# A transformer kernel: the last mixer in reusable 8 KB buffers, operands at a fixed distance in SBUF, and the scatter moved within the expert

## The chip, the cores and the metric

One core of a Trainium2 chip runs the kernel. The metric is the device time in microseconds, taken as the median of three runs. Each run is one launch that goes from inputs in HBM to the output in HBM.

## The reference

256 tokens of width 1024 go through two blocks, all in float32. The first block has two layers; each is a SwiGLU FFN (hidden width 2816), a mixer and a second FFN. The second block has a third mixer and a mixture of 32 experts.

```python
for i in range(2):
    x = x + 0.5 * swiglu(rmsnorm(x), ffn1[i])
    x = x + (gla_mixer if i == 0 else sb_mixer)(rmsnorm(x))
    x = x + 0.5 * swiglu(rmsnorm(x), ffn2[i])
h = rmsnorm(x)                       # second block
proj = rms_norm(h) @ w_in            # conv input, two gates, q, k, v
h = h + concat([short_conv(...), diff_attention(...)]) @ w_out
hn = rms_norm(h)
# each token: the best of 4 groups, the best 2 of its 8 experts
for e in range(32):
    y += (silu(hn @ gate[e]) * (hn @ up[e]) * comb[:, e]) @ down[e]
return h + y
```

Every weight is used once, so 393 MB have to come from HBM: 180 tiles of 1 MB for the dense part (four FFNs, three mixers) and 192 tiles, six for each expert (four of gate and up, two of down).

## The kernel before

**The dense part.** Everything lies transposed, channels on the 128 partitions and 256 tokens along them. Each float32 operand is cut into a high and a low float32r part, and `mm3` makes a product of three matmuls: high weights with the high and the low part of the tokens, low weights with the high part. The tokens are `hhi` and `hlo`. A weight tile is loaded into `raw`, ScalarE copies the high part to `whi`, VectorE the rest to `wlo`; each of the three names has a ring of four buffers of 128 x 2048. The class `Feed` goes through a list of all tiles (`weight_plan`) in the order of use. `gu` matmuls take `hhi`, `hlo`; down takes `ahi`, `alo` (the activated gate times up) and accumulates in `acc`; projections of the mixers are `pj`; `pv` are the value projections, in which the tokens are the weights and the weight tile is streamed. The output projections `acco` take `ohi`, `olo` in the first two mixers and `mhi`, `mlo` in the third.

**Where the operands lie.** Tiles get their place in SBUF one after the other in the order in which the code makes them, and a pool starts behind the pools that are open. In the built program `whi` and `wlo` lie at multiples of 512 bytes. Every operand of a product is a slice at a multiple of 512 bytes in its tile, so the distance from weights to moving operand, modulo 512, is the same for all products of one pair of tiles:

| moving operand | where | distance modulo 512 |
|---|---|---|
| `hhi`, `hlo` | all `gu` and `pj` | 480 |
| `ahi`, `alo` | down of FFNs 1 to 3 | 192 |
| `ahi`, `alo` | down of FFN 4 (the pool `late` is open) | 64 |
| `ohi`, `olo` | output projection of the first mixer | 384 |
| `ohi`, `olo` | output projection of the second mixer | 192 |
| `mhi`, `mlo` | output projection of the third mixer | 64 |
| the weight tile, with `hhi` as weights | `pv` | 32 |

**The expert part.** An expert's tile isn't split: it goes as it is into any free buffer of 8 KB a partition, and the matmuls are float32. `Feed.load` issues the loads, all on SP's queue and in the list's order; each waits on the queue until its buffer is free. After the last dense tile, the buffers come one after the other: the four of `raw` as the last dense tiles are split, `whi` and `wlo` as the last output projection leaves them (`feed.done`), four `wx` of a pool that opens when the third mixer's pool is closed, and `h32` and `xT` when the router has read them. From then on each expert tile that has been used hands its buffer back:

```python
w = feed.take(("gx", "w_exp", e, j))
...
feed.add([w])
```

The third mixer `mix2` has the tensors `q2`, `k2`, `sq2`, `vt2`, `yT`, `oT`, `mhi`, `mlo`, four `p`, `u` and small ones in its own pool. In the expert loop `gate_up(e)` makes the gate and up products of the tokens gathered for expert e (`gx`, from `xg`), `act(s)` transposes and activates, `down(e, a)` gives `yy`, and `scatter(e - 1, ...)` adds the expert before to the accumulators with eight matmuls, after `gate_up(e)` is complete. The order on each engine is the order of the code (`manual_schedule`).

Of the kernel before, what the change touches and what calls it, by code (L numbers as in the profile page):

```python
# [14 lines left out]
OP = mybir.AluOpType  # L15
# [10 lines left out]
NE = 32  # L26
SL = 32
# [164 lines left out]
class Feed:  # L192
# [5 lines left out]
    def __init__(self, nc, pool, wts, plan):  # L198
        self.nc, self.pool, self.wts, self.plan = nc, pool, wts, plan
        self.M = sum(k[0] not in ("gx", "dx") for k in plan)  # L200
        self.raw, self.cut, self.free = {}, {}, []
        self.nl = self.ns = self.at = 0

    def part(self, name, dtype):

        return self.pool.tile([P, TW], dtype, name=name, tag=name, bufs=self.RING)
# [84 lines left out]
def body(ctx, tc, xin, small, cst, masks, groups, wts, out):  # L291
# [12 lines left out]
    ct = base.tile([P, cwid], F32, name="ct")  # L304
    g0 = base.tile([P, ND], F32, name="g0")
    feed = Feed(nc, base, wts, plan)
    nc.sync.dma_start(out=g0, in_=small[:, 0:ND])
# [15 lines left out]
    ones = base.tile([P, 2], F32, name="ones")  # L323
# [3 lines left out]

    hhi = base.tile([P, ND, T], F32R, name="hhi")
    hlo = base.tile([P, ND, T], F32R, name="hlo")
    ssq = base.tile([P, 2, 512], F32, name="ssq")  # L330
    rt = base.tile([P, 2], F32, name="rt")
    rb = base.tile([P, T], F32, name="rb")
# [278 lines left out]
    def gla(gnext):  # L611
        with tc.tile_pool(name="gla", bufs=1) as pool, tc.tile_pool(name="glaa", bufs=1, space=PS) as pacc:
# [332 lines left out]
    def mix2(gnext):  # L945
        with tc.tile_pool(name="mix", bufs=1) as pool:
            half2["pool"] = plate
            H4 = (P, 4, T)
            qk = [pool.tile(H4, F32, name=n) for n in ("q2", "k2")]
            sq = pool.tile(H4, F32, name="sq2")  # L950
            vt = pool.tile([P, 2, 512], F32, name="vt2")
            yT = pool.tile(H4, F32, name="yT")
            oT = pool.tile(H4, F32, name="oT")
            mhi = pool.tile([P, ND, T], F32R, name="mhi")
            mlo = pool.tile([P, ND, T], F32R, name="mlo")
            cb = pool.tile([P, 2, P], BF16, name="cb2")
            rb1, rbb = ssq[:, 1, :T], ssq[:, 1, T:]
            sel = pool.tile([2 * ND, ND * P], F32, name="sel")
            nc.sync.dma_start(out=sel, in_=groups)
            nlam = pool.tile([P, 4], F32, name="nlam")  # L960
            gq = pool.tile([P, 2], F32, name="gq")
            rt1 = pool.tile([P, 2], F32, name="rt1")
            nc.gpsimd.tensor_copy(cb[:, 0, :], ident)
            nc.gpsimd.tensor_copy(cb[:, 1, :], C("negc"))
            rb2 = rb[:, None, :].to_broadcast([P, 2, T])
            half = C("half")
            g1 = S("final_norm")

            def pair(b):
                return b.rearrange("p (s t) -> p s t", s=2)  # L970

            def stats2():
                ms = bank("ms")
                for k, src in ((0, ssq[:, 0, :]), (1, ssq2)):
                    for tb in range(2):
                        for h in range(2):
                            o = h * T + tb * P
                            mm(ms[:, 2 * k + tb:2 * k + tb + 1], lhsT=src[:, o:o + P], rhs=one, start=(h == 0), stop=(h == 1))

                v = pool.tile([P, 4], F32, name="v4")  # L980
                nc.vector.tensor_scalar(v[:, 0:2], ms[:, 0:2], 1.0 / D, EPS, op0=OP.mult, op1=OP.add)
# [694 lines left out]
```

## Time and profile before

| | before |
|---|---|
| median of three runs | 1607.97 us (1607.24 to 1608.25) |
| the profiled execution, its own time | 1605.98 us |
| its span, first to last instruction | 1603.8 us |
| TensorE busy | 1448.3 us, 90% |
| VectorE busy | 782.6 us, 49% |
| ScalarE busy | 570.1 us, 36% |
| DMA | 395.60 MB, 247 GB/s over the span |
| mean granted TensorE clock | 0.953 |

Busy is the time in which an engine runs at least one instruction. Matmuls overlap one another, so a matmul's duration (some 280 ns) is longer than the time from one start to the next; a busy share near 1 means that TensorE always has work, not that it works as fast as it can. The span is 2.2 us shorter than the execution's own time.

### The profile page before, as it was taken

Reading aid. Unit: us, or ns where it says so; the run is one execution under the profiler, and the core shown is the slowest. Engines: PE = TensorE matmul, PEld = TensorE weight load, DVE = VectorE, ACT = ScalarE, POOL = GpSimd, SP = SyncE. Lnnn points to the kernel's source line nnn. Section 1 sums busy time; section 2 is a strip of 40 time slices with the busy share of each in tenths; the row PEclk is TensorE's granted clock in tenths of the full one; section 3 lists DMA queues with packets and bytes.
Section 4 is the critical chain, followed back from the end, with each engine's and each line's share of the span. In section 5 each row is a group of like instructions: output and inputs, shape, how many; then the busy total and the mean of one; then the engine's idle time right before and its main releaser. Section 6 shows DMA issues by size and latency. Waiting matters only on the chain.

```text
span 1603.8 us, 31147 instructions
## 1 busy us (share of the span) xinstructions
PE 1448.3 (90%) x13785; PEld 1271.2 (79%) x13785; DVE 782.6 (49%) x1163; ACT 570.1 (36%) x708; POOL 52.8 (3%) x53
## 2 busy tenths in 40 slices
PE   8999999999999999999999999999996676676665
PEld 8999999999999999999999999998752332242322
DVE  6765677766566656563466556877310110110001
ACT  5444455454444544455554444544210000000000
POOL 0000013100000000000010000100000000000000
PEclk9999999999999999999999999999898888878888
DMA  7645544245544555543345555424999999999996
GB/s 288 240 183 187 188 158 159 98 179 198 200 174 154 225 190 189 184 171 120 132 141 210 202 178 185 157 89 150 421 423 424 424 424 424 423 424 423 424 424 283
DMA packets 56475, 395.60 MB, mean 247 GB/s; under 512 B 6401, under 2 KB 6657, under 8 KB 8977
## 3 DMA queue, kind: packets, MB, share of 16 engines
q1 hardware_dynamic: 56336, 393.57, 63.3%
q8 instruction: 110, 1.80, 0.4%
q14 instruction: 29, 0.23, 0.0%
HBM read 392.50 MB, written 1.05 MB: 245 GB/s over the span
## 4 chain that ended last, share of the span: by engine, by line
PE 66%; DMA 26%; DVE 4%; ACT 3%; issue 1%; SPq 0%; ACTq 0%
DMA wlo<-wts 12%; PE gu L442 10%; PE gu L440 10%; PE gu L441 10%; DMA raw<-wts 9%; PE acc L440 5%; PE acc L441 5%; PE acc L442 5%; DMA wx<-wts 4%; PE pj L440 3%; PE pj L441 3%; PE pj L442 3%; DMA xT<-wts 1%; DVE wlo L252 1%; PE gx L1473 1%; ACT whi L249 1%
## 5 line engine op out<-in xcount | busy, mean ns | idle before, releaser
L252 DVE TENSOR_TENSOR wlo<-raw,whi 128x2048 fp32r<-128x2048 f32 (+1 forms) x186 | 413.3, 2232 | 205.4 <-ACT whi L249 205.4
L440 PE MATMUL gu<-hhi,whi 128*128 128x256 f32 x1408 | 397.4, 282 | 6.9 <-ACT whi L249 6.9
L442 PE MATMUL gu<-hhi,wlo 128*128 128x256 f32 x1408 | 397.1, 282 | 1.5 <-DVE wlo L252 1.5
L441 PE MATMUL gu<-hlo,whi 128*128 128x256 f32 x1408 | 396.6, 282 | 0.0
L249 ACT ACTIVATE whi<-raw 128x2048 fp32r<-128x2048 f32 (+1 forms) x186 | 342.5, 1855 | 51.0 <-issue 40.9
L440 PEld LDWEIGHTS gu<-hhi,whi 128*128 128x128 f32 x1408 | 266.3, 189 | 6.9 <-ACT whi L249 6.9
L442 PEld LDWEIGHTS gu<-hhi,wlo 128*128 128x128 f32 x1408 | 266.3, 189 | 2.5 <-DVE wlo L252 2.5
L441 PEld LDWEIGHTS gu<-hlo,whi 128*128 128x128 f32 x1408 | 266.4, 189 | 0.0
L440 PE MATMUL acc<-ahi,whi 128*128 128x256 f32 x704 | 195.7, 278 | 0.0
L441 PE MATMUL acc<-alo,whi 128*128 128x256 f32 x704 | 195.4, 278 | 0.0
L442 PE MATMUL acc<-ahi,wlo 128*128 128x256 f32 x704 | 195.2, 277 | 0.0
L1510 DVE TENSOR_SCALAR pt<-ptb,ct 128x256 f32<-128x256 f32 x32 | 15.5, 484 | 306.4 <-PE ptb L1508 306.4
L1477 ACT ACTIVATE gs<-gx 128x256 f32<-128x256 f32 x32 | 12.3, 384 | 366.7 <-PE gx L1473 366.7
L480 ACT ACTIVATE sg<-gp 128x256 f32<-128x256 f32 x88 | 36.8, 418 | 294.4 <-DVE gp L479 289.8
L442 PEld LDWEIGHTS acc<-ahi,wlo 128*128 128x128 f32 x704 | 132.5, 188 | 0.0
L440 PEld LDWEIGHTS acc<-ahi,whi 128*128 128x128 f32 x704 | 132.4, 188 | 0.0
L441 PEld LDWEIGHTS acc<-alo,whi 128*128 128x128 f32 x704 | 132.1, 188 | 0.0
L440 PE MATMUL pj<-hhi,whi 128*128 128x256 f32 x416 | 120.2, 289 | 0.0
L441 PE MATMUL pj<-hlo,whi 128*128 128x256 f32 x416 | 118.5, 285 | 0.6 <-DVE hlo L391 0.6
L442 PE MATMUL pj<-hhi,wlo 128*128 128x256 f32 x416 | 118.1, 284 | 0.0
L1473 PE MATMUL gx<-raw,xg 128*32 128x256 f32 x704 | 59.0, 467 | 41.6 <-DMA raw<-wts 40.5
L1473 PE MATMUL gx<-wx,xg 128*32 128x256 f32 x640 | 56.3, 490 | 32.2 <-DMA wx<-wts 32.2
(383 smaller groups left out, 2069.3 us busy)
## 6 DMA issues: line engine op xcount, KB each, us to landing
raw<-wts SPq DMA_DIRECT2D x222, 1024.0 KB, 4.8
whi<-wts SPq DMA_DIRECT2D x44, 1024.0 KB, 19.7
wlo<-wts SPq DMA_DIRECT2D x44, 1024.0 KB, 19.7
wx<-wts SPq DMA_DIRECT2D x40, 1024.0 KB, 19.6
h<-wts SPq DMA_DIRECT2D x10, 1024.0 KB, 19.7
xT<-wts SPq DMA_DIRECT2D x10, 1024.0 KB, 19.7
raw<-wts SPq DMA_DIRECT2D x8, 256.0 KB, 5.9
xT<-xin SPq DMA_DIRECT2D x4, 256.0 KB, 5.2
```

Source lines behind the costliest of these rows:

```text
L249: self.nc.scalar.activation(hi[:, o], r[:, o], AF.Copy)
L252: self.nc.vector.tensor_sub(lo[:, o], r[:, o], hi[:, o].bitcast(F32))
L440: mm(o, lhsT=whi, rhs=xhi, start=start, stop=False, skip_group_check=True)
L441: mm(o, lhsT=whi, rhs=xlo, start=False, stop=False, skip_group_check=True)
L442: mm(o, lhsT=wlo, rhs=xhi, start=False, stop=stop, skip_group_check=True)
L480: nc.scalar.activation(sg, gp, AF.Silu)
L1473: mm(b[rows[q], :W], lhsT=x[:, c, e % 8, :], rhs=w[:, o:o + W], start=(c == 0), stop=(c == ND - 1), skip_group_check=True)
L1477: nc.scalar.activation(s, b[:, :W], AF.Copy)
L1510: V.tensor_scalar(pt, b[:, :T], C("slot"), None, op0=OP.is_equal)
```

## The change

It has three parts. The diff is shown without its changes of indentation.

**Places in SBUF.** All tiles of the dense part are made in an order, with gaps, that puts the moving operand 192 bytes (modulo 512) behind the weights in all `mm3` products. The scratch for DMA descriptors shrinks from 16 KB to 2 KB a partition. In the program after, `whi` and `wlo` lie at 416 modulo 512, and `hhi`, `hlo`, `ahi`, `alo`, `ohi`, `olo`, `mhi`, `mlo` at 96; in `pv` the distance is 320.

```diff
     ct = base.tile([P, cwid], F32, name="ct")
+    parts = {n: base.tile([P, TW], d, name=n, tag=n, bufs=Feed.RING) for n, d in (("raw", F32), ("whi", F32R),
+                                                                                   ("wlo", F32R))}
     g0 = base.tile([P, ND], F32, name="g0")
+    ones = base.tile([P, 2], F32, name="ones")
+    rt = base.tile([P, 2], F32, name="rt")
+    for n in ("nv2", "ny2", "nt2"):
+        base.tile([P, 2], F32, name=n, tag=n, bufs=2)
+    base.tile([P, GAP], F32, name="gap")
+    hhi = base.tile([P, ND, T], F32R, name="hhi")
+    hlo = base.tile([P, ND, T], F32R, name="hlo")
...
+            pool.tile([P, 80], F32, name="gap")
             ohi = pool.tile([P, ND, T], F32R, name="ohi")
...
+    late.tile([P, 80], F32, name="gap0")
+    late.tile([P, 2, 8, SL], F32R, name="pq", tag="pq", bufs=1)
+    late.tile([P, 80], F32, name="gap1")
...
-    nc = bacc.Bacc("TRN2", target_bir_lowering=False, num_devices=1)
+    nc = bacc.Bacc("TRN2", target_bir_lowering=False, num_devices=1, dynamic_dma_scratch_size=SCRATCH)
```

**Buffers of 8 KB in the third mixer.** Its tensors become eight slabs: `sA` (q and k), `sB` (`sq`, `oT`), `sC` (`yT`, `vt`), `sD` and `sE` (`mhi`, `mlo`, later the two `xg`), `sF` (two of the `p`, `u`), `sG` (the other two `p`, `rqT`), and `sX`, which holds nothing of the mixer. The pool stays open until the end. All but `sD` and `sE` are handed to `Feed` as the mixer is done with them; `wx` is gone. With `raw`, `whi`, `wlo`, `h32` and `xT` that makes 20 buffers in place of 18.

```diff
+    def slab(pool, name, dtype=F32):
+        return pool.tile([P, TW], dtype, name=name, tag=name, bufs=1)
+
+        mhi = slab(pool, "sD", F32R).rearrange("p (c t) -> p c t", c=ND)
+        mlo = slab(pool, "sE", F32R).rearrange("p (c t) -> p c t", c=ND)
+        qk, (sq, oT), (yT, vt) = [[t[:, k * 1024:(k + 1) * 1024].rearrange("p (h t) -> p h t", h=4) for k in range(2)]
+                                  for t in (slab(pool, "sA"), slab(pool, "sB"), slab(pool, "sC"))]
+        sp = [slab(pool, "sF"), slab(pool, "sG")]
+        feed.add([slab(pool, "sX")])
...
         conv_c(1, u, next_heads, lambda: held.update(p=differences(held["p"])))
+        feed.add([slab(pool, "sA"), slab(pool, "sF")])
...
         aT += [turned(2 + h, x) for h, x in enumerate(p)]
+        feed.add([slab(pool, "sG")])
...
         value(1, sums, last_heads)
+        feed.add([slab(pool, "sC")])
...
             out_norm(2, r23)
+            feed.add([slab(pool, "sB")])
...
-        feed.add([pool.tile([P, TW], F32, name=f"wx{i}") for i in range(4)])
```

SP's queue at the end of the dense loads, before. The rows are loads in the order of issue; `raw` x14 are the last ten dense tiles and the first four of the experts.

```order
L959 DMA sel<-groups 16x1024
L223 DMA raw<-wts 128x2048 x14
L223 DMA whi<-wts 128x2048
L223 DMA wlo<-wts 128x2048
L223 DMA whi<-wts 128x2048
L223 DMA wlo<-wts 128x2048
L223 DMA whi<-wts 128x2048
L223 DMA wlo<-wts 128x2048
L223 DMA whi<-wts 128x2048
L223 DMA wlo<-wts 128x2048
L223 DMA wx_12387<-wts 128x2048
L223 DMA wx_12388<-wts 128x2048
```

The same place after; the ten `raw` are dense, and all from `sX` on are experts' tiles.

```order
L971 DMA sel<-groups 16x1024
L227 DMA raw<-wts 128x2048 x10
L227 DMA sX<-wts 128x2048
L227 DMA sA<-wts 128x2048
L227 DMA sF<-wts 128x2048
L227 DMA raw<-wts 128x2048
L227 DMA sG<-wts 128x2048
L227 DMA raw<-wts 128x2048 x2
L227 DMA sC<-wts 128x2048
L227 DMA raw<-wts 128x2048
L227 DMA sB<-wts 128x2048
L227 DMA whi<-wts 128x2048
```

Ten loads of experts stand ahead of the first `whi`, where four stood. The two `raw` behind `sG` and the one behind `sC` now wait behind those loads' own waits.

**The scatter.** It goes into `gate_up`, ahead of the last of the four gate and up tiles. The tiles `gs` and `pt` become slices of one tile `gp`.

```diff
                 feed.add([w])
+                if j == 2 and held_y:
+                    scatter(e - 1, *held_y.pop())
...
             s = gate_up(e)
-            if held_y is not None:
-                scatter(e - 1, *held_y)
             pt = where(e)
             a = act(s)
             next(steps, None)
-            held_y = pt, down(e, a)
+            held_y.append((pt, down(e, a)))
```

TensorE's queue in the second expert, before (`gx` is gate and up, eight matmuls a row; `acc` and `lb` are the accumulators of the scatter, `ptb` and `gt` what follows gate and up).

```order
L1473 MATMUL gx<-whi,xg 32x256 x8
L1473 MATMUL gx<-wlo,xg 32x256 x8
L1473 MATMUL gx<-whi,xg 32x256 x8
L1473 MATMUL gx<-wlo,xg 32x256 x8
L1516 MATMUL acc<-pt,yy 128x256 x2
L1516 MATMUL lb<-pt,yy 128x256 x2
L1516 MATMUL acc<-pt,yy 128x256 x2
L1516 MATMUL lb<-pt,yy 128x256 x2
L1508 LDWEIGHTS idb
L1508 MATMUL ptb<-svT,idb 128x256
L1484 MATMUL gt<-ct,gs 128x128 x2
```

The same place after.

```order
L1492 MATMUL gx<-raw,sD 32x256 x8
L1492 MATMUL gx<-sC,sD 32x256 x8
L1492 MATMUL gx<-raw,sD 32x256 x8
L1537 MATMUL acc<-gp,yy 128x256 x2
L1537 MATMUL lb<-gp,yy 128x256 x2
L1537 MATMUL acc<-gp,yy 128x256 x2
L1537 MATMUL lb<-gp,yy 128x256 x2
L1492 MATMUL gx<-sB,sD 32x256 x8
L1529 LDWEIGHTS idb
L1529 MATMUL ptb<-svT,idb 128x256
L1505 MATMUL gt<-ct,gp 128x128 x2
```

The eight scatter matmuls moved ahead of the expert's last eight gate and up matmuls. All other instructions stand in the same order on TensorE, VectorE, ScalarE and GpSimd as before.

## Rows read from the trace of the kernel before

**Rows 1.** The page's slices: TensorE's busy tenths and DMA's GB/s, 40 slices.

```profile
PE   8999999999999999999999999999996676676665
...
GB/s 288 240 183 187 188 158 159 98 179 198 200 174 154 225 190 189 184 171 120 132 141 210 202 178 185 157 89 150 421 423 424 424 424 424 423 424 423 424 424 283
```

**Rows 2.** Windows: us; busy PE, PEld, DVE, ACT, POOL; clock, DMA share, GB/s.

```profile
200.00:400.00 200.00, 198.29 (x1665) 195.75 (x1664) 141.29 (x193) 97.62 (x102) 26.87 (x24) 1.00 0.44 158
...
1200.00:1300.00 100.00, 68.88 (x917) 32.70 (x909) 11.03 (x26) 4.84 (x14) 0.00 (x0) 0.83 1.01 424
```

**Rows 3.** The page's groups: xcount, busy us, mean ns, idle before.

```profile
L440 PE MATMUL gu<-hhi,whi 128*128 128x256 f32 x1408 | 397.4, 282 | 6.9 <-ACT whi L249 6.9
...
L440 PE MATMUL acc<-ahi,whi 128*128 128x256 f32 x704 | 195.7, 278 | 0.0
...
L440 PE MATMUL pj<-hhi,whi 128*128 128x256 f32 x416 | 120.2, 289 | 0.0
```

**Rows 4.** Tile gu, 174.4 to 185.8 us: ns min/median/max, starts.

```profile
L440 PE MATMUL gu<-hhi,whi x32: 277/280/285, 174.5 to 185.5; 128*128 128x256 f32 x32
...
L442 PE MATMUL gu<-hhi,wlo x32: 277/280/285, 174.7 to 185.7; 128*128 128x256 f32 x32
```

**Rows 5.** Tile acc, end of the first FFN, 185.8 to 196.7 us.

```profile
L440 PE MATMUL acc<-ahi,whi x32: 276/276/286, 185.8 to 196.4; 128*128 128x256 f32 x32
...
L442 PE MATMUL acc<-ahi,wlo x32: 276/276/282, 186.1 to 196.6; 128*128 128x256 f32 x32
```

**Rows 6.** Tile acc, end of the fourth FFN, 992.3 to 1003.6 us.

```profile
L440 PE MATMUL acc<-ahi,whi x32: 280/280/281, 992.3 to 1003.3; 128*128 128x256 f32 x32
...
L442 PE MATMUL acc<-ahi,wlo x32: 279/279/279, 992.6 to 1003.5; 128*128 128x256 f32 x32
```

**Rows 7.** Tile acco, output projections of the first and second mixer.

```profile
L440 PE MATMUL acco<-ohi,whi x64: 274/281/383, 295.9 to 319.7; 128*128 128x256 f32 x64
...
L440 PE MATMUL acco<-ohi,whi x64: 276/276/384, 786.0 to 813.4; 128*128 128x256 f32 x64
```

**Rows 8.** Tile pv, all of the dense part.

```profile
L599 PE MATMUL pv<-whi,hhi x160: 277/280/384, 225.2 to 1100.8; 128*128 128x256 f32 x160
```

**Rows 9.** Timeline of SP's queue: start us, us, what.

```profile
1091.62 0.33 SPq L223 DMA_DIRECT2D raw<-wts  x1
...
1093.82 0.33 SPq L223 DMA_DIRECT2D raw<-wts  x1
...
1119.30 0.33 SPq L223 DMA_DIRECT2D whi<-wts  x1
...
1144.74 0.33 SPq L223 DMA_DIRECT2D xT<-wts  x1
1153.26 0.33 SPq L223 DMA_DIRECT2D raw<-wts  x1
```

**Rows 10.** Issues at 1091.62, 1144.74, 1153.26; last column us to landing.

```profile
raw<-wts SPq DMA_DIRECT2D x1, 1024.0 KB, 4.7
...
xT<-wts SPq DMA_DIRECT2D x1, 1024.0 KB, 12.9
...
raw<-wts SPq DMA_DIRECT2D x1, 1024.0 KB, 6.9
```

**Rows 11.** The chain that ended last: start us, us, what.

```profile
1106.92 0.43 DVE mlo L1094
...
1118.05 0.43 DVE mlo L1094
```

**Rows 12.** Timeline of TensorE in the last expert.

```profile
1587.41 1.92 PE L1473 MATMUL gx<-wlo,xg 128*32 128x256 f32 x16 [0.50 <-DMA wlo<-wts]
...
1589.26 0.48 PE L1516 MATMUL acc<-pt,yy 32*128 32x256 f32 x2
...
1590.42 0.44 PE L1484 MATMUL gt<-ct,gs 128*128 128x128 f32 x2
...
1591.55 1.07 PE L1498 MATMUL y<-whi,sg 128*32 128x256 f32 x16 [0.69 <-DVE sg L1488]
```

More of the change, by code (lines that the diff above doesn't have):

```diff
@@ new lines, in conv_c, with conv_b, gated @@
+            proj_t(("col", "w_in_2", 0, c_w + g * 256), convolve, ahead=2 if g else None)
+        def conv_b(g, last=None):
+            bs = h32[:, 6:8, :]
+            y = yT[:, 2 * g:2 * g + 2, :]
+            def gated(b):
+                scaled(bs)(b)
+                nc.vector.tensor_mul(y, y, bs)
+                nc.scalar.activation(bs, y, AF.Square)
+                if last is not None:
+                    last()
+            proj_t(("col", "w_in_2", 0, 512 + g * 256), gated)
+            return bs
@@ new lines, in out_sums, with out_norm @@
+        def out_sums(h0):
+            os = bank("os")
+            for h in range(2):
+                for tb in range(2):
+                    i = 2 * h + tb
+                    mm(os[:, i:i + 1], lhsT=sq[:, h0 + h, tb * P:(tb + 1) * P], rhs=one, start=True, stop=True)
+            return rsqrt(pool, os[:, :4], 4, 1.0 / P, "rp")
+        def out_norm(h0, r):
+            b = bank("ob")
+            for h in range(2):
+                spread(b[:, h * T:(h + 1) * T], lambda tb: r[:, 2 * h + tb:2 * h + tb + 1])
+            for h in range(2):
+                bb = b[:, h * T:(h + 1) * T]
+                nc.vector.scalar_tensor_tensor(oT[:, h0 + h, :], oT[:, h0 + h, :], gq[:, 1:2], bb, op0=OP.mult,
+                                               op1=OP.mult)
+                cut(4 + h0 + h, oT[:, h0 + h, :])
@@ new lines, in mix2 @@
+        u = conv_x(0)
+        residual(2)
+        ss = bank("ss")
+        for n, src in enumerate((sq, oT)):
+            for c in range(4):
+                group_sums(ss, 8, 4 * n + c, src[:, c, :])
+        r = rsqrt(pool, ss[:, :32], 32, 1.0 / 64, "rq")
+        conv_c(0, u, lambda: held.update(rq=rows64(r, 8, "rqT")))
+        ysq = conv_b(0)
+        bq = [banks("qb") for _ in range(2)]
+        for c in range(4):
+            for n in range(2):
+                spread64(bq[c // 2][:, c % 2, n * T:(n + 1) * T], held["rq"], 8, 4 * n + c)
@@ new lines, in mix2, with next_heads @@
+        for c in range(4):
+            for n in range(2):
+                nc.vector.scalar_tensor_tensor(qk[n][:, c, :], qk[n][:, c, :],
+                                               gq[:, 0:1] if n == 0 else S("k_norm_g_2"),
+                                               bq[c // 2][:, c % 2, n * T:(n + 1) * T], op0=OP.mult, op1=OP.mult)
+        u = conv_x(1)
+        p = head_scores(0)
+        rc0 = conv_sums(0, ysq)
+        p = differences(p)
+        def next_heads():
+            held["rc"] = rows64(rc0, 2, "rcT")
+            held["p"] = head_scores(2)
+            held["aT"] = [turned(h, x) for h, x in enumerate(p)]
@@ new lines, in last_heads, with tail @@
+        def last_heads():
+            b = conv_spread(held["rc"])
+            head_out(2, aT[2])
+            head_out(3, aT[3])
+            conv_norm(1, b)
+        value(1, sums, last_heads)
+        feed.add([slab(pool, "sC")])
+        r23 = out_sums(2)
+        def tail():
+            out_norm(0, held["r01"])
+            yield
+            out_norm(2, r23)
+            feed.add([slab(pool, "sB")])
+            yield
+            residual(3)
+        out_proj("w_out_2", lambda c: (mhi[:, c, :], mlo[:, c, :]), gnext, early=[0, 1, 2, 3], mid=tail(), last=True)
```

492 lines of the change are left out of this document (210 added, 282 removed).

## The prediction, made before the change was run

> **What bounds the kernel now.** I read the slices of the page first, then the windows, then the page's groups, then single tiles. The slices [rows 1] show two kernels in one. For about 1120 us the core moves 89 to 288 GB/s and TensorE is busy throughout; for the last 470 us it moves 421 to 424 GB/s in every full slice and TensorE has gaps. The windows say the same in numbers [rows 2]: TensorE has 198.3 us busy of 200 in the stretch with the first mixer, and 68.9 us of 100 in the expert part, where the DMA engines are full (share 1.01). So the dense part is worth what its matmuls cost, and the expert part is worth when its stream of loads starts and how many loads are then left.
>
> Three groups carry the dense part: gate and up (`gu`), down (`acc`), projections (`pj`), three lines each, of which [rows 3] shows one: 3 x 1408 = 4224, 3 x 704 = 2112, 3 x 416 = 1248 matmuls, all of 128x128 weights and 256 columns. The last column of these rows tells what TensorE waited for just before them: 6.9 us for `gu`, on ScalarE's split of a weight tile, and nothing for the other two. So a nanosecond on each dense matmul reaches the end almost whole.
>
> **Part one, the addresses.** Before, `acc` has a shorter mean duration than `gu` (278 against 282 ns in [rows 3]) at the same shape and the same three lines of `mm3`. Looking closer, the same down projection runs at two speeds. At the end of the first FFN its median is 276 ns, and its 96 matmuls start between 185.8 and 196.6 us [rows 5]: 10.8/95 = 113.7 ns from one to the next. At the end of the fourth FFN, same code, the median is 279 to 280 and they take 992.3 to 1003.5 us [rows 6]: 11.2/95 = 117.9 ns. `gu` has 280 ns, 174.5 to 185.7 us, again 117.9 ns [rows 4]. What differs is the place in SBUF, which the section on the kernel lists: moving operand minus weights, modulo 512 bytes, is 192 in the first three FFNs' down, 64 in the fourth's, 480 in `gu` and `pj`. The output projections repeat it: 281 ns at 384 (first mixer), 276 ns at 192 (second) [rows 7]. Four distances, and 276 ns at 192 alone. The change puts all of these at 192.
>
> The sum for this part, at 117.9 - 113.7 = 4.2 ns (the medians, 280 to 276, say 4):
> `gu` 4224 x 4.2 = 17.7 us; `pj`, at the same distance as `gu`, 1248 x 4.2 = 5.2; the fourth FFN's down, 528 x 4.2 = 2.2; the first mixer's output projection, 192 x 5 (281 to 276) = 1.0; the last mixer's, at 64 like the fourth FFN, 192 x 4.2 = 0.8. Together 26.9 us. The rest of `acc` and the second mixer's output projection stay at 192 and gain nothing.
> `pv` has its operands the other way round and goes from 32 to 320, which no row shows. It has 280 ns now [rows 8]; between the extremes seen, 276 and 281, its 480 matmuls are worth -1.9 to +0.5 us. I take 0: 320 is as far from 192 as 64 is.
> TensorE's waits for VectorE and ScalarE hang on work that does not get shorter, and some will grow as TensorE speeds up. In the FFNs the splits run tiles ahead, so this touches the mixers alone, where 1.7 us of 200 are idle now [rows 2]; I take off 1.0 us. Part one: -25.9 us, bounds -23 and -31 (half a nanosecond either way on 6400 starts, `pv` with its own bounds); a reading that is wrong altogether is among the rivals.
>
> [...]
>
> **Part two, the loads.** Before, the last dense load is issued at 1091.62 us, expert load 1 at 1093.82, and by 1119.30, when the first `whi` is handed over, four are out [rows 9]. Then come eight into `whi` and `wlo`, four into `wx`, then `h32` and `xT`: 18 buffers, all issued by 1144.74. The next load needs a buffer that an expert has used, and that comes free at 1153.26, set by TensorE's first expert and not by loads. At that point the queue still works on `xT`, whose load took 12.9 us [rows 10] and lands at 1157.6; load 19, issued at 1153.26, took 6.9 us and lands at 1160.2.
>
> After, six more loads go out before 1119.30 (`sX`, `sA`, `sF`, `sG`, `sC`, `sB`) and the four `wx` are gone: 20 buffers. The mixer's order on its engines is unchanged, so I keep its times. `sX` can leave only behind the last dense load (SP issues in order), at 1092; the readers of `sA` and `sF` are done by then. `sC` and `sB` wait for the last splits of the normalised convolution and heads, which end at 1107.4 and 1118.5 us [rows 11]. What is queued behind those two waits on SP is only expert loads, which nobody needs before 1152. Bandwidth is there: 11 loads of 1.05 MB at 424 GB/s [rows 2], 2.47 us each, are 27 us, the stretch from 1092 to 1119. So the queue runs dry soon after `xT` (1144.74 + 4.7 = 1149.4), and load 21 starts at 1153.26 on an idle queue: 4.7 us, as the last dense load had on one [rows 10], so it lands at 1158.0. Before, load 21 lands at 1160.2 + 2 x 2.47 = 1165.1. From there both streams are equally full (424 GB/s, page's slices [rows 1]), so the end moves by 1165.1 - 1158.0 = **7.1 us**: 4.9 for two more buffers, 2.2 for a queue without a backlog. The six early loads do not count as six: four take the place of `wx`, and the queue then stands still for some 4 us. Bounds: 4.9 (the backlog stays) and 11 (the 4 us of standstill close too, as they would if a buffer came free when `xT` lands).
>
> **Part three, the scatter.** Eight matmuls of expert e-1 move ahead of expert e's last gate-up tile. In the stream TensorE waits there for that tile, so they fill a wait. At the end the timeline [rows 12] shows what is left: the last gate-up tile at 1587.41, the scatter from 1589.26, the transposes at 1590.42, down at 1591.55. Without the scatter between, transposes and down can start up to 0.7 us sooner (they still wait for the copy of `gx`), but the second half of down needs the last load, which comes when it comes. Bounds 0 and 0.7; I take 0.2, near the load. The smaller descriptor scratch and the shared tiles `gp` and `rcT` move no instruction: 0.
>
> Sum: -25.9 - 7.1 - 0.2 = **-33.2 us**. The profiled execution took 1605.98 us, so 1572.8 for one like it; the median of the three runs, 1607.97, is 2.0 above it, so **1574.8 us**.
>
> **The rivals.**
> 1. Addresses do nothing for `gu` and `pj`; the two speeds of down have some other cause. For: [rows 4] and [rows 5] are different code. Against: [rows 5] and [rows 6] are the same, and `acco` repeats it. Then only parts two and three: 1607.97 - 7.3 = 1600.7. [...]
> 2. Slower: it is not the distance that counts but the moving operand's own address. Before, the weights always lie at 0 modulo 512, so distance and address cannot be told apart in `gu`, `acc`, `acco`; after, weights lie at 416 and moving operands at 96, where no fast row lies. Then 1584 down matmuls lose 4.2 ns (6.7 us) and 192 of the second mixer 5 (1.0); if in addition the 6000 others go from 280 to the 281 of [rows 7], 6.0 more. That is +13.7 - 7.3 = +6.4: 1614.4. It is slower than now as soon as what is lost passes 7.3 us, that is if these 1776 fall back and the others get any worse.
> 3. TensorE gets its 4 ns, but VectorE, 141 us busy of 200 in the first mixer's stretch [rows 2], sets the pace outside the FFNs, and half of part one is swallowed: 1607.97 - 20 = 1587.8. Against it: the waits in [rows 3] are small.
> 4. The early loads bring nothing, because the stream then loses as much elsewhere: 1607.97 - 26.1 = 1581.9. Against it: the stream's rate is the same in every full slice.
>
> **How the numbers follow.** Chances: forecast 0.74 (its own range 1566 to 1582), rival 3 0.08, rival 4 0.05, rival 1 0.06, rival 2 0.07. The range 1564 to 1592 takes in the forecast, with the bounds of both parts, and rivals 3 and 4, and leaves out rivals 1 and 2 with a tail: under 0.2. A measurement of this kernel can tell about 0.2% (3.2 us) from no change. All cases but rival 2 are faster by more than that; of rival 2, part lies within 0.2%. Faster 0.90, same 0.04, slower 0.06.
>
> **What would show it.** Right: `gu` and `pj` at a median of 276 ns; the fourth FFN ending about 24 us earlier than 1003.5 us (all but the last mixer's share of part one); 10 expert loads issued before the first `whi`; the queue idle before the first reused buffer, and no idle time after it. Wrong in part one: `gu` still at 280, or `acc` of the first FFN at 279. Wrong in part two: load 21 landing less than 5 us sooner, counted from the first expert's start, or new waits of SP ahead of `raw`. What would upset all of it: the clock falling in the dense part, where the granted share is now 1.00 [rows 2].

## The result, and the profile after

| | before | after |
|---|---|---|
| median | 1607.61 us (4 runs, 1605.12 to 1608.25) | 1584.49 us (4 runs, 1580.62 to 1587.87) |
| ratio, 95% interval | | 0.9858 (0.9829 to 0.9888) |
| the profiled execution, own time | 1605.98 us | 1587.87 us |
| its span | 1603.8 us | 1585.5 us |

The changed kernel is 23 us faster where 33 were forecast. Of the profiled executions the one after is the slowest of its four and the one before lies 1.6 us below its median, so the spans differ by only 18.3 us.

The page's slices, as in [rows 1].

```profile
PE   8999999999999999999999999999996676676665
...
GB/s 291 236 189 187 186 144 166 98 171 229 200 184 159 224 192 213 185 161 127 114 160 213 187 187 186 162 81 318 342 420 420 421 421 419 421 421 420 421 420 286
```

In its full slices the stream now has 419 to 421 GB/s where it was 421 to 424. The page's groups, as in [rows 3].

```profile
L449 PE MATMUL gu<-hhi,whi 128*128 128x256 f32 x1408 | 394.8, 280 | 7.3 <-ACT whi L253 7.3
...
L449 PE MATMUL acc<-ahi,whi 128*128 128x256 f32 x704 | 196.0, 278 | 0.0
...
L449 PE MATMUL pj<-hhi,whi 128*128 128x256 f32 x416 | 118.4, 285 | 0.0
```

`gu` went from 282 to 280 ns, not by the 4 expected, and `acc` has not moved. The windows of the four FFNs and of the stream tell why (columns as in [rows 2]).

```profile
7.00:197.50 190.50, 189.94 (x1592) 189.52 (x1593) 125.26 (x157) 90.65 (x102) 3.25 (x3) 1.00 0.60 221
319.00:499.30 180.30, 180.30 (x1592) 180.30 (x1591) 117.33 (x147) 84.86 (x88) 1.29 (x1) 1.00 0.55 198
499.40:679.90 180.50, 180.50 (x1594) 180.50 (x1594) 118.49 (x149) 84.63 (x89) 2.59 (x2) 1.00 0.52 193
800.50:991.20 190.70, 189.45 (x1593) 188.87 (x1592) 120.98 (x151) 88.96 (x95) 2.94 (x6) 0.99 0.54 194
...
1200.00:1300.00 100.00, 67.31 (x810) 30.50 (x810) 9.75 (x23) 5.54 (x15) 0.00 (x0) 0.86 1.01 421
```

The same 1592 matmuls, at a granted clock of 0.99 to 1.00, take 180 us in FFNs 2 and 3 and 190 in FFNs 1 and 4. Single tiles, as in [rows 4] to [rows 6]: `gu` late in FFN 1 and in FFN 2, `acc` at the end of FFNs 1, 2 and 4.

```profile
L449 PE MATMUL gu<-hhi,whi x32: 281/281/282, 175.0 to 186.0; 128*128 128x256 f32 x32
...
L449 PE MATMUL gu<-hhi,whi x26: 276/276/277, 479.7 to 488.2; 128*128 128x256 f32 x26
...
L450 PE MATMUL acc<-alo,whi x32: 281/281/282, 186.4 to 197.4; 128*128 128x256 f32 x32
...
L449 PE MATMUL acc<-ahi,whi x32: 276/276/277, 488.6 to 499.1; 128*128 128x256 f32 x32
...
L449 PE MATMUL acc<-ahi,whi x32: 281/281/281, 980.0 to 990.9; 128*128 128x256 f32 x32
```

All of these lie at distance 192, and `gu` uses the same `hhi`, `hlo`, `whi` and `wlo` in every FFN. Yet there are two paces, a pace being the time from the start of one matmul to the start of the next: 113.3 ns and 117.8 ns, almost without scatter (112 to 115, and 116 to 120). Over the 1584 matmuls of an FFN these 4.5 ns are up to 7 of the 10 us; the rest lies at the start of FFNs 1 and 4, which take 182 to 185 us at the fast pace too (d112 and best in the table below). `acc` of FFN 1, which had the fast pace [rows 5], has lost it. TensorE's timeline where FFN 1 changes pace:

```profile
38.68 0.28 PE L451 MATMUL acc<-ahi,wlo 128*128 128x256 f32 x1
38.80 0.28 PE L449 MATMUL gu<-hhi,whi 128*128 128x256 f32 x1
38.91 0.28 PE L450 MATMUL gu<-hlo,whi 128*128 128x256 f32 x1
39.45 0.38 PE L451 MATMUL gu<-hhi,wlo 128*128 128x256 f32 x1 [0.26 <-DVE wlo L256]
39.67 0.28 PE L449 MATMUL gu<-hhi,whi 128*128 128x256 f32 x1
39.79 0.28 PE L450 MATMUL gu<-hlo,whi 128*128 128x256 f32 x1
39.91 0.28 PE L451 MATMUL gu<-hhi,wlo 128*128 128x256 f32 x1
```

Up to 38.91 us the starts are 0.11 apart. One wait of 0.26 us for `wlo` breaks the row, and behind it they are 0.12 apart for the rest of the FFN. Behind the first dozen matmuls of a row, in which it settles, no pace in these FFNs changed without such a break or a change of operands.

The loads, as in [rows 9] and [rows 10]; first SP's timeline, then the issue at 1137.29 with its time to landing.

```profile
1076.34 0.33 SPq L227 DMA_DIRECT2D raw<-wts  x1
1076.72 0.42 SPq L227 DMA_DIRECT2D sX<-wts  x1
...
1103.26 0.33 SPq L227 DMA_DIRECT2D sB<-wts  x1
1104.02 0.33 SPq L227 DMA_DIRECT2D whi<-wts  x1
...
1129.04 0.33 SPq L227 DMA_DIRECT2D xT<-wts  x1
1137.29 0.33 SPq L227 DMA_DIRECT2D sX<-wts  x1
1139.00 0.33 SPq L227 DMA_DIRECT2D sA<-wts  x1
```

```profile
sX<-wts SPq DMA_DIRECT2D x1, 1024.0 KB, 4.7
```

Ten loads of experts precede the first `whi`, and load 21 finds an empty queue and takes 4.7 us, as forecast. The first reused buffer comes free at 1137.29 in place of 1153.26 [rows 9]: 16.0 us earlier, where part one promised 25.9.

The stages, each from the end of the one ahead, from the starts and landings in the traces of this kernel and of those below (us):

```
              FFN1   mix1   FFN2   FFN3   mix2   FFN4   mix3  router  first gx   load 30    last load
                                                                      to load 30 to last    to end
before       189.7  123.3  186.2  186.2  121.5  189.9  127.8   20.4     36.5      403.9      11.6
after        190.2  121.3  180.5  180.5  120.4  190.9  124.4   20.4     31.6      406.9      11.0
again        190.5  121.3  180.5  180.5  120.9  190.6  125.1   20.2     32.0      406.8      11.2
far480       189.6  122.4  186.2  186.2  121.7  187.7  128.8   20.4     30.2      407.0      11.2
aligned      185.1  121.9  180.8  180.5  120.6  184.2  131.2   20.3     30.6      401.5      12.5
buf18        185.4  121.1  180.5  180.5  120.4  189.3  124.5   19.5     35.8      407.3      11.0
scat_back    191.4  121.3  180.5  180.5  120.4  184.2  131.6   20.3     31.1      406.9      11.3
d112         184.6  121.3  180.6  180.5  120.9  182.3  125.3   20.4     30.6      406.9      11.1
d112_b       184.9  121.3  180.6  180.5  120.4  182.7  128.0   20.4     30.4      406.9      11.1
best         184.8  121.3  180.6  180.5  121.1  183.9  130.8   20.4     29.9      401.7      12.1
best_b       184.0  121.3  180.6  180.5  121.1  182.3  130.8   20.4     30.6      401.5      11.1
before112    185.1  122.3  181.3  181.3  121.2  184.7  129.5   20.4     35.6      405.2      11.8
```

### The profile page after: what moved, and what is told of

It reads as the page before. It is cut to its first block, busy times and chain, and to the rows that moved or that the text cites. A ratio compares the mean times of both kernels' runs of the same rounds, so it can differ in the third digit from the quotient of the medians.

```text
span 1585.5 us, 31150 instructions
## 1 busy us (share of the span) xinstructions
PE 1431.3 (90%) x13785; PEld 1249.2 (79%) x13785; DVE 781.4 (49%) x1163; ACT 569.1 (36%) x708; POOL 52.8 (3%) x53
## 4 chain that ended last, share of the span: by engine, by line
PE 68%; DMA 23%; DVE 5%; ACT 3%; issue 1%; SPq 0%; ACTq 0%
PE gu L451 10%; PE gu L449 10%; PE gu L450 10%; DMA raw<-wts 7%; DMA whi<-wts 6%; PE acc L451 5%; PE acc L449 5%; PE acc L450 5%; DMA sX<-wts 4%; PE pj L449 3%; DMA sF<-wts 3%; PE pj L450 3%; PE pj L451 3%; DMA h<-wts 2%; PE gx L1492 2%; DVE wlo L256 1%
## 5 line engine op out<-in xcount | busy, mean ns | idle before, releaser
L1531 DVE TENSOR_SCALAR gp<-ptb,ct 128x256 f32<-128x256 f32 x32 | 15.5, 483 | 281.7 <-PE ptb L1529 281.7
L1498 ACT ACTIVATE gp<-gx 128x256 f32<-128x256 f32 x32 | 12.3, 383 | 393.7 <-PE gx L1492 393.7
L450 PE MATMUL pj<-hlo,whi 128*128 128x256 f32 x416 | 116.7, 280 | 0.7 <-DVE hlo L400 0.7
L450 PEld LDWEIGHTS pj<-hlo,whi 128*128 128x128 f32 x416 | 79.3, 191 | 0.9 <-DVE hlo L400 0.9
L449 PEld LDWEIGHTS pj<-hhi,whi 128*128 128x128 f32 x416 | 79.1, 190 | 1.0 <-issue 1.0
```

The lines of the kernel that those rows point to most:

```text
L449: mm(o, lhsT=whi, rhs=xhi, start=start, stop=False, skip_group_check=True)
L450: mm(o, lhsT=whi, rhs=xlo, start=False, stop=False, skip_group_check=True)
L1498: nc.scalar.activation(s, b[:, :W], AF.Copy)
L1531: V.tensor_scalar(pt, b[:, :T], C("slot"), None, op0=OP.is_equal)
```

## The experiments

Theory A: at distance 192 a row of dense matmuls has two steady paces, takes one of them when it starts, and keeps it until a wait or another matmul breaks the row. Its rivals: the pace belongs to the stage (theory B), the distance alone decides (the prediction), or the moving operand's own address does (rival 2 of the prediction).

**again.** The changed kernel, unaltered.

> The changed kernel once more, unaltered. Theory A, two paces: at distance 192 a row of dense matmuls runs either at 113.3 or at 117.8 ns from start to start, keeps that pace until something interrupts the row, and takes one of the two anew behind the interruption. Then FFNs 2 and 3, which the same matmuls interrupt at their start, come out at 113.3 again, FFNs 1 and 4 may come out either way, each worth 1584 x 4.4 ns = 7.0 us, and executions differ by up to 7 us or more (the first ones did: 1580.6 to 1587.9). Theory B, the pace belongs to the stage: FFNs 1 and 4 at 117.8 and FFNs 2 and 3 at 113.3 in every execution, and executions differ by about 3 us as those of before did (1605.1 to 1608.3).

1586.71 us (4 runs, 1584.67 to 1590.30; ratio 0.9869, 0.9849 to 0.9888). FFNs 1 and 4 have 117.8 ns again, so this trace does not tell A from B. The two traces differ in detail: here FFN 1 fell to 117.8 at 24.9 us, behind the matmuls of the norm's spread, not at 39.7.

**micro.** The disputed cost by itself: the same triple of matmuls, 48 to a block, with slices of one tile as the moving operand.

```diff
+    kicks = [None, spread, None, stats, spread, lambda: short(32), lambda: short(64), lambda: short(96),
+             lambda: short(128), lambda: short(160), lambda: short(192), lambda: short(224)]
...
+    for a, d in [(0, d) for d in DIST] + [(a, 192) for a in ABS]:
+        for kick in kicks:
+            if kick:
+                kick()
+            gu(f"g{a}d{d}q", a, d)
```

> The disputed cost by itself; it computes nothing of the reference and hands the input through. Blocks of 48 matmuls as in gate and up (high and low weights, 256 columns), at ten distances from 0 to 480 with the weights at one address, and at distance 192 with three other weight addresses; between the blocks nothing, or a short matmul of one of nine kinds. Theory A (two paces): at 192 blocks of 113.3 and blocks of 117.8 ns, constant within a block, changing only behind a short matmul; at 480 about 118.3 whatever stands ahead; at 64 117.8. Theory of the prediction (distance alone): at 192 113.3 to 113.7 in every block, 117.8 or more at all others. Rival 2 (the moving operand's own address): at 192 the blocks with other weight addresses differ from the first. Rival 1 (addresses do nothing): one pace at all distances.

The tiles of the blocks at distances 64, 480 and 192 (names end in the distance), then three pieces at 192: the first block, one behind another matmul, one behind a matmul of 96 columns.

```profile
L50 PE MATMUL g0d64q<-xh,wh x192: 279/279/365, 98.9 to 168.5; 128*128 128x256 f32 x192
...
L50 PE MATMUL g0d480q<-xh,wh x192: 277/281/365, 589.8 to 659.7; 128*128 128x256 f32 x192
...
L50 PE MATMUL g0d192q<-xh,wh x192: 276/281/364, 239.6 to 308.5; 128*128 128x256 f32 x192
...
L50 PE MATMUL g0d192q<-xl,wh x16: 276/276/283, 239.7 to 244.9; 128*128 128x256 f32 x16
...
L50 PE MATMUL g0d192q<-xh,wl x15: 281/281/281, 263.8 to 268.7; 128*128 128x256 f32 x15
...
L50 PE MATMUL g0d192q<-xh,wl x16: 276/276/279, 280.7 to 285.8; 128*128 128x256 f32 x16
```

The means from start to start in ns, one for each of the 11 rows between two breaks at a distance, without the first dozen matmuls of a row:

```
distance 0, 256    120.0 in all 22
distance 64, 320   117.8 in all 22
distance 128, 384  118.5 to 120.1
distance 480       118.3 in all 11
distance 32        116.7 in 8, 117.8 in 3
distance 192       113.3 117.8 113.3 117.8 117.8 117.8 113.3 117.8 117.8 117.8 113.3
distance 448       the same sequence as 192
192, other weight addresses (+128, +256, +384): both paces again, 113.3 in 7, 3 and 5 of 11
```

Theory A holds: at 192 the same operands run at either pace, the pace changes only behind another matmul, and the row keeps it. What selects it is not shown. The kind of matmul ahead alone does not: behind the one of 32 columns the rows at the four weight addresses have 117.8, 113.3, 117.8 and 117.8. The paces themselves go with the distance modulo 256, and at 192 all four weight addresses have the same two; rival 2 falls, and so does "192 is fast". That addresses matter at all is plain at 0: 120.0 against 113.3 ns, with no other engine and no load at work. So with no other engine at work the pace depends on how the two operands lie to one another; why it does is not shown.

**far480.** `hhi` and `hlo` back at distance 480, the rest as in the change.

```diff
-    base.tile([P, GAP], F32, name="gap")
+    base.tile([P, GAP + 72], F32, name="gap")
...
+    base.tile([P, 56], F32, name="gap2")
```

> The changed kernel with hhi and hlo moved to distance 480, where they lay before; everything else stays (down and output projections at 192, buffers, scatter). Prediction's reading (192 fast, 480 slow): gate, up and projections go back to 118 ns, slower than the changed kernel by 5472 x 4.2 = 23 us: 1607. Theory A (two paces at 192): gate and up lose 0.5 ns in FFNs 1 and 4 and 5 ns in 2 and 3 (11.6 us), projections about 5 us, and down of FFNs 1 and 4 gets 4.1 ns x 1056 = 4.3 us back: slower by about 12, near 1597. Rival 1 (addresses do nothing for gate, up and projections): the same time, 1584.

1599.17 us (ratio 0.9944, 0.9929 to 0.9960), 12.5 above the changed kernel on the same chip: A's 12, not 23 and not 0. By stages (table above) the four FFNs are 7.6 us longer than in the trace of again, where A gives 7.3; of the 3.7 us in the third mixer 3.4 are the clock, by an estimate (10.2 us at a granted clock of 0.50 against 3.4, half of the difference counted as lost). Late in FFN 1, `gu` and then `acc`:

```profile
L450 PE MATMUL gu<-hhi,whi x32: 277/280/285, 173.8 to 184.8; 128*128 128x256 f32 x32
...
L450 PE MATMUL acc<-ahi,whi x32: 276/276/286, 185.2 to 195.7; 128*128 128x256 f32 x32
```

This is the picture of before. `gu` at 480 has one pace, 118.3, and each block of `acc` behind it starts afresh and finds 113.3. With both at 192 a slow `gu` hands its pace on to `acc`: 281 ns in both at the end of FFN 1 in the changed kernel.

**aligned.** Everything from `raw` on 96 bytes further, and the slabs behind `sE` 320 more: weights at 0, moving operands at 192, and 18 of the 20 buffers at multiples of 512.

```diff
+    base.tile([P, 24], F32, name="gap0")
     parts = {n: base.tile([P, TW], d, name=n, tag=n, bufs=Feed.RING) for n, d in (("raw", F32), ("whi", F32R),
...
+        pool.tile([P, 80], F32, name="gap2")
         qk, (sq, oT), (yT, vt) = [[t[:, k * 1024:(k + 1) * 1024].rearrange("p (h t) -> p h t", h=4) for k in range(2)]
```

> The changed kernel with weights at 0 and moving operands at 192 modulo 512 (96 bytes further on, distance still 192), and with 16 of the 20 buffers at multiples of 512 bytes (raw, whi, wlo, sA, sB, sC, sF, sG, sX make 18, h32 and xT lie off). Distance is what counts: the dense part has the same two paces as now and ends within 7 us of the changed kernel's. Rival 2 (the moving operand's own address, 192 being the good one): FFNs 1 and 4 go to 113.3 to 113.7 ns as well, 14 us faster. In the stream: if the buffer's place counts for a load (before, loads into whi and wlo, at multiples of 512, landed 2.44 to 2.46 us apart, those into raw, wx, h32 and xT 2.49 to 2.52), loads land 2.45 us apart in place of 2.48 and the stream ends about 5 us sooner; if it does not, 2.48 again.

1581.15 us (ratio 0.9827, 0.9808 to 0.9846). In this trace FFNs 1 and 4 both came out at 113.3, which rival 2 had asked for; but buf18 gets the same in FFN 1 and scat_back in FFN 4, without moving an operand of the dense part. The stream gains what was expected: load 30 to the last 401.5 us in place of 406.8. Two windows of the stream:

```profile
1200.00:1300.00 100.00, 65.84 (x797) 30.70 (x789) 10.86 (x25) 5.82 (x16) 0.00 (x0) 0.88 1.01 426
1300.00:1550.00 250.00, 169.63 (x2227) 77.26 (x2227) 23.70 (x57) 12.42 (x36) 0.00 (x0) 0.86 1.01 426
```

**buf18.** Two buffers fewer.

```diff
-        feed.add([slab(pool, "sX")])
...
-            feed.add([slab(pool, "sB")])
```

> The changed kernel with sX and sB not handed to the loads: 18 buffers as before, 8 early loads. Measured from the first expert's first matmul. Prediction's term (a buffer is one load of 2.47 us): the last load lands 4.9 us later than with 20 buffers, 443.4 in place of 438.5 us behind that matmul. Rival (the gain of more buffers is given back in the stream, since the changed kernel's last load lands only 2.0 us sooner by this measure than before's, 438.5 against 440.5): 0 to 2 us later. In the whole time: 5 us, or 0 to 2, on top of 7 us for each FFN that comes out at the other pace.

From the first `gx` to the last landing 443.1 us; the traces after, again, far480, scat_back and d112, with 20 buffers off multiples of 512, have 437.2 to 438.8, mean 438.0. So 5.1 us for two buffers: the prediction's term, and the rival falls. The whole time, 1586.76 (1577.99 to 1598.96), hides this behind the paces. FFN 1 of this kernel, whose dense part has the changed kernel's addresses:

```profile
L449 PE MATMUL gu<-hhi,whi x14: 276/276/276, 159.8 to 164.2; 128*128 128x256 f32 x14
```

276 here and 281 there, at the same places. This is what theory B cannot have.

**scat_back.** The scatter behind gate and up again.

```diff
-                if j == 2 and held_y:
-                    scatter(e - 1, *held_y.pop())
...
             s = gate_up(e)
+            if held_y:
+                scatter(e - 1, *held_y.pop())
```

> The changed kernel with the scatter behind the whole of gate and up again. Prediction's term: 0.2 us, between 0 and 0.7, to be read from the last landing to the end of the span: 11.0 us with the scatter moved, 11.6 in before; so 11.2 to 11.7 here. Rival (the scatter's place costs or gives something in the stream, because a buffer is freed behind it): the stretch from the first expert's first matmul to the last landing, 438.5 to 438.8 us with the scatter moved, changes by more than 1 us.

From the last landing to the end 11.34 us, against 11.01 to 11.23 in the traces after, again, far480, buf18 and d112, with the scatter moved. That is 0.2 us above their mean, but from one trace: best and best_b below, which are one kernel, have 12.05 and 11.07 us there. So this trace does not tell 0.2 from nothing. The stretch ahead of it is 437.95 us, within theirs, so the rival falls. The whole time (1587.40, ratio 0.9870, 0.9837 to 0.9903) cannot tell it from the changed kernel. `acc` of FFN 4, again at unchanged addresses:

```profile
L450 PE MATMUL acc<-alo,whi x32: 276/276/276, 974.0 to 984.6; 128*128 128x256 f32 x32
```

**micro2.** Finer distances, and loads into buffers at six places.

```diff
+    for p in PUT:
+        o = ((p - OFF) % 512) // 4
+        for k in range(NL):
+            nc.sync.dma_start(out=bufs[k % NB][:, o:o + TW], in_=wts[k])
```

> Computes nothing of the reference and hands the input through. First the blocks of 48 matmuls with short matmuls between them, at fourteen finer distances (multiples of 16 bytes, and 184, 200, 216 around 192). The first such run gave the same pace at a distance and at that distance plus 256, so distance modulo 256 should decide here too: below 192 mixtures of 117.8 and 120, above 192 up to 118.3 at 224. Open is whether some distance gives 113.3 in every block, whatever stands ahead; theory A does not exclude one, and the prediction's theory names 192 alone. Beside it 240 loads of 1 MB on SP's queue, ten buffers in turn, 40 loads each to places 0, 64, 96, 128, 256 and 416 modulo 512. Alignment theory: 2.44 to 2.45 us from one landing to the next at 0, 2.48 to 2.49 at 96, 128 and 416. Rival (the loads' pace comes from the order of buffers or from the readers): the same at all six.

One distance has a single fast pace, 112: 113.3 ns in nine rows of 11; in the other two the mean over the same stretch is 113.8, as these settle a few matmuls later, at 113.3 too. The other thirteen have slow rows (16: 113.3 to 118.7; 208: 116.7 to 119.2; 184, 200 and 216, around 192, all 119.9 to 120.9). The tile at 112:

```profile
L51 PE MATMUL g0d112q<-xh,wh x192: 275/275/367, 309.8 to 377.5; 128*128 128x256 f32 x192
```

The windows of the six places, in the order 0, 64, 96, 128, 256, 416 (columns busy PE, PEld, ACT, POOL, then clock, DMA share, GB/s):

```profile
20.00:100.00 80.00, 80.00 (x685) 80.00 (x685) 0.00 (x0) 0.00 (x0) 1.00 1.01 426
115.00:200.00 85.00, 85.00 (x718) 85.00 (x718) 0.00 (x0) 0.00 (x0) 1.00 1.01 420
215.00:300.00 85.00, 85.00 (x714) 85.00 (x713) 0.00 (x0) 0.00 (x0) 1.00 1.01 421
315.00:400.00 85.00, 85.00 (x741) 85.00 (x740) 0.00 (x0) 0.00 (x0) 1.00 1.01 420
420.00:500.00 80.00, 80.00 (x681) 80.00 (x680) 0.00 (x0) 0.00 (x0) 1.00 1.01 426
515.00:600.00 85.00, 85.00 (x717) 85.00 (x716) 0.00 (x0) 0.00 (x0) 1.00 1.01 421
```

At 0 and 256 the median from one landing to the next is 2.44 us, at the others 2.48 to 2.49. So of these places the two at multiples of 256 are the fast ones, and neither the order of buffers nor their readers are needed for it. Here the places written are the ones that differ; why some are slow no run shows.

**d112, best, before112.** d112 puts `hhi`, `hlo`, `ahi`, `alo` at 112 modulo 256 from the weights; best is the same on the aligned kernel; before112 is the kernel before with `hhi` and `hlo` alone moved. The distances between tiles in these programs are multiples of 32 bytes, so 112 needs a slice that starts inside its tile. The core of the edit:

```diff
-    hhi = base.tile([P, ND, T], F32R, name="hhi")
+    hhi = base.tile([P, TW + 64], F32R, name="hhi")[:, 4:4 + TW].rearrange("p (c t) -> p c t", c=ND)
...
-                hi = pool.tile([P, T], F32R, name="ahi", bufs=7)
+                hi = pool.tile([P, T + 64], F32R, name="ahi", bufs=7)[:, 44:44 + T]
```

> The changed kernel with hhi, hlo, ahi and alo at distance 112 modulo 256 in place of 192; output projections stay at 192. In the second run of blocks by themselves 112 gave 113.3 ns whatever stood ahead. Theory A: all four FFNs at 113.3 ns; FFN 1 takes 185 us and FFN 4 184 us from the end of what stands ahead to its last matmul, as they do where they came out at 113.3 at distance 192, against 190 to 191 in the changed kernel: 12 us less. The third mixer took 131 us with its clock falling four times in the kernels whose FFN 4 was fast, and 124 where it was not, so up to 7 us of this may be lost again: 1575 to 1582. The executions lie closer together. Rival (in the whole kernel something else than the distance picks the pace, such as the loads or the other engines, which the blocks by themselves lacked): 117.8 ns appears again in FFN 1 or 4, and the time stays at 1585.

> The same distance 112, with the weights and 18 of the 20 buffers at multiples of 512 bytes as in the aligned kernel. Theory A and alignment: the dense part as in d112, and loads 2.44 to 2.45 us apart in place of 2.48, which is 5 to 6 us over the stream: 1569 to 1577. Rival (one gain eats the other, the loads' readers being late): no more than 2 us faster than d112.

> The kernel before with hhi and hlo alone moved, from distance 480 to 112; buffers, order of loads, scatter and all else as before. The addresses alone: gate and up 4224 x (118.3 - 113.3) = 21 us and projections 1248 x 4.5 = 6 us less, value projections 0.7 more (144 in place of 32): 1581; with 7 us lost to the clock in the third mixer 1588. Rival 1 (addresses do nothing for gate, up and projections): 1607.

| kernel | median us | ratio | 95% interval |
|---|---|---|---|
| d112 | 1580.07 (1573.38 to 1582.09) | 0.9827 | 0.9809 to 0.9845 |
| best | 1572.82 (1570.91 to 1576.01) | 0.9786 | 0.9770 to 0.9801 |
| before112 | 1587.89 (1587.02 to 1590.89) | 0.9884 | 0.9867 to 0.9902 |

d112, `gu` late in FFN 1 and `acc` at the end of FFN 4:

```profile
L450 PE MATMUL gu<-hhi,whi x14: 275/275/275, 159.8 to 169.7; 128*128 128x256 f32 x14
...
L450 PE MATMUL acc<-ahi,whi x32: 275/275/275, 966.1 to 976.7; 128*128 128x256 f32 x32
```

All four FFNs have the fast pace, in this kernel, in best, and `gu` in before112. before112 shows the addresses alone: 19.3 us up to the first `gx`, though its third mixer had 13.7 us at half clock where before had 6.8; rival 1 of the prediction falls. best beats the changed kernel. Its median lies 7 us below d112's, but d112's five times spread over 8.7 us, and in the two traces the gain does not reach the end: load 30 to the last takes 5.2 us less, the third mixer 5.5 us more, and the spans are 1573.6 and 1571.1 us. One expectation failed: the times of d112 lie no closer together (1573.4 to 1582.1) than those of the changed kernel.

**d112_b, best_b.** The same two kernels for a second trace.

> The kernel d112 once more, for a second trace. Theory A: all four FFNs at 113.3 ns again (185, 180.5, 180.5 and 182 to 184 us). The third mixer had one fall of the clock and 125.3 us in the first trace of this kernel, four falls and 129.5 to 131.6 us in four other kernels. If that is decided by each execution, its five times (1573.4 to 1582.1, a spread that the FFNs no longer explain) come from there, and this trace has either 125 us with one fall or 130 with several. If it is set by the kernel's code, 125.3 again, and the spread has another cause.

> The kernel best once more, for a second trace. All four FFNs at 113.3 ns again; from the load that lands as number 30 to the last 401 to 402 us again, 5 us less than with buffers off multiples of 512. Third mixer 131 us again if its code sets the falls of the clock, 125 or 131 if each execution does.

1575.80 and 1573.95 us, one execution each; the FFNs have the fast pace again. The third mixer varies: 125.3 us in d112, 128.0 in d112_b, 130.8 in both of best. Windows in the changed kernel, its third mixer and the stretch in it at half clock:

```profile
991.20:1115.60 124.40, 121.32 (x988) 114.72 (x987) 88.89 (x199) 57.34 (x103) 8.37 (x8) 0.99 0.50 198
...
1027.50:1030.90 3.40, 3.40 (x18) 3.40 (x18) 1.60 (x9) 0.00 (x0) 0.00 (x0) 0.50 0.72 289
```

The same in best:

```profile
978.70:1109.50 130.80, 127.78 (x988) 121.23 (x987) 89.81 (x201) 58.30 (x105) 8.89 (x8) 0.93 0.50 188
...
987.20:994.00 6.80, 6.80 (x33) 6.80 (x33) 4.96 (x18) 2.46 (x2) 0.00 (x0) 0.50 0.00 0
1017.90:1021.30 3.40, 3.40 (x18) 3.40 (x17) 1.99 (x11) 0.00 (x0) 0.00 (x0) 0.50 0.90 299
1035.00:1038.40 3.40, 3.40 (x19) 3.40 (x18) 3.40 (x6) 1.14 (x1) 0.00 (x0) 0.50 0.17 31
1062.30:1065.70 3.40, 3.40 (x18) 3.40 (x17) 1.85 (x5) 2.26 (x4) 0.00 (x0) 0.50 0.00 0
```

The same 988 matmuls, with the granted clock at 0.50 for 3.4 us in the one and for 17.0 in the other. By the same records it was 3.4 us in d112, 10.2 in d112_b, and some 17 in best_b, aligned and scat_back. Half of 17.0 - 3.4 is 6.8 us (an estimate from the granted 0.50), which is what aligned and scat_back lose there against the changed kernel (131.2 and 131.6 against 124.4). d112 and d112_b are one kernel, so the executions differ, and their times with them. Ahead of the falls at 1027.5 (changed kernel) and 1017.9 (best) TensorE had been busy for the whole of 6.8 us. Ahead of the one at 987.2 in best it had been busy for 5.67 of 6.8 us with 47 matmuls; in d112 the same 47 matmuls took 5.66 of 6.8 us (978.7 to 985.5), and no fall came. What sets it is open.

## Why the prediction was right or wrong

The time, 1584.5, fell in the range and the sign was right; the sum was 10 us too large. That the range held is in part luck: the forecast's own range, 1566 to 1582, missed, and the stated one reached to 1592 to take in rivals 3 and 4, whose reasons did not bring the miss of part one.

**Part one, -25.9, measured -15.8** (first `gx` at 1151.75 before, 1135.99 after). By stages:

| | FFN 1 | mixer 1 | FFN 2 | FFN 3 | mixer 2 | FFN 4 | mixer 3 |
|---|---|---|---|---|---|---|---|
| forecast | -4.4 | -2.6 | -4.4 | -4.4 | -1.6 | -6.6 | -2.8 |
| after | +0.5 | -2.0 | -5.6 | -5.6 | -1.0 | +1.0 | -3.4 |
| d112 | -5.1 | -2.0 | -5.6 | -5.7 | -0.5 | -7.5 | -2.5 |

The forecast took another 1.0 off for waits; the first `gu` started 0.4 us later than before. Two entries of after hold the clock as well, with half of the time at a granted clock of 0.50 counted as lost, an estimate: FFN 4 had 3.4 us at half clock (809.1 to 812.5), before none, a loss of 1.7; the third mixer had 3.4 us where before had 6.8 (1039.6 to 1043.0 and 1056.7 to 1060.1), a gain of 1.7. In the sum the two cancel, but only half of the third mixer's 3.4 us is the change's. The granted clock of 1.00 that the prediction names for the dense part is that of its stretch in [rows 2], not of the third mixer. The step that failed is "Four distances, and 276 ns at 192 alone. The change puts all of these at 192", read as if 192 were enough. At 192 there are two paces, and the slow one, 117.8, is no better than where `gu` came from. FFNs 1 and 4 got it and gave 0.5 and 1.0 us away in place of 4.4 and 6.6 gained; `acc` of FFN 1 fell with `gu`, a loss that the prediction had only under rival 2. Where the fast pace came, the term was too small: 118.3 to 113.3 is 5.0 ns, not 4.2. The rows of before could have warned. [rows 7] gives the second mixer's output projection at 192 a median of 276 ns; in that trace it began at 117.8 and changed within the stage. A median of one stage does not show a second pace in it.

`pv`, put at 0, did not measurably move: median 280 before [rows 8], 279 to 280 after.

**Part two, -7.1, measured -2.0** (first `gx` to last landing, 440.5 to 438.5). The mechanism was right: ten early loads, an idle queue, and load 21 lands 6.0 us behind the first `gx` in place of 13.6, 7.6 sooner. The other traces with these 20 buffers off multiples of 512 have -1.6 to -3.3. Two buffers are worth 5.1 (forecast 4.9). The step that failed is "From there both streams are equally full". By load 30 only 4.9 us are left (4.5 to 6.3 in those other traces): buffers come free singly (1137.29, 1139.00), and loads 21 and 22 land 4.3 us apart. From load 30 to the last another 2.95 go. There the change took the eight of 18 buffers that lay at multiples of 512, `whi` and `wlo`, off them; 162 loads x 8/18 x 0.045 us is 3.2, an estimate from the landings (2.44 us against 2.48 to 2.49 in micro2). It is not sharper than 1 to 2 us: before112, with the places of before, took 405.2 there and not 403.9, with seven loads that landed over 2.9 us behind the one ahead where before had three. This is rival 4 in part; the argument against it, the even 424 GB/s, was the rate of a mixture of places. Why loads 21 and 22 lie so far apart on an empty queue stays open.

**Part three, -0.2:** by scat_back too small to tell from nothing. From the last landing to the end the profiled spans differ by 0.5.

Together -15.8 - 2.0 - 0.5 is the 18.3 us of the spans. Rival 1 is refuted by before112 and far480, rival 2 by micro. Rivals 3 and 4 gave totals nearer to 1584.5 than the forecast's (1587.8 and 1581.9). Rival 4 was right on most of part two. Rival 3 (VectorE swallows half of part one) had the wrong reason: FFNs 2 and 3 took the full gain, and what is missing is missing in the FFNs at a slower pace of TensorE itself. What would have shown part one right, FFN 4's end 24 us earlier, did not: it was 12.3. "`gu` still at 280, or `acc` of the first FFN at 279" did show it wrong.

## What to carry to other kernels

A steady row of float32r matmuls can have several paces at one and the same pair of addresses (113.3 and 117.8 ns at 192 here): look at the start times over whole stages, not at a median, and measure a distance behind several kinds of break before building on it. Of the 19 distances tried here (modulo 256), 112 was the only one that came to the fast pace, 113.3 ns, in every row. Put buffers that a full stream fills at multiples of 256 bytes (in micro2 a load of 1 MB took 2.44 us there, 2.48 to 2.49 at four other places), and check what an edit for one purpose does to the places of the rest: here the gap that served the matmuls cost the stream some 3 us (406.9 from load 30 to the last, 403.9 before), and with both set right the kernel takes 1572.8 us.

## What the runs showed of the hardware that was not expected

- The pace of 128x256 float32r matmuls goes with (moving operand - weights) modulo 256: 113.3 ns at best, 120.9 at worst (216), at a granted clock of 1.00. At 192 a row keeps one of two paces (113.3 and 117.8), and at 16 (113.3 to 118.7), 32 (116.7 and 117.8), 128 (118.5 to 120.1) and 208 (116.7 to 119.2) the rows do not all have one pace either. Why is not shown.
- A load of 1 MB in a full stream lands 2.44 us (median) after the one ahead into buffers at 0 or 256 modulo 512, and 2.48 to 2.49 into those at 64, 96, 128 and 416.
- The granted clock fell to 0.50 in the third mixer, where TensorE is busy 97 to 98% of the time, for 3.4 us in one execution (d112) and 10.2 in another of the same kernel (d112_b).
